# Gate rows made one by one between groups of gathered expert rows

## The chip, the core and the metric

One core of a Trainium2 chip runs one launch of the whole program. The metric is the device time of the launch in microseconds (us); a kernel is run several times and the median counts.

## The reference, cut to what matters

256 tokens of 1024 features pass a first block (a mixer and a retrieval layer) and a second block of two attention layers, with a context of 256 tokens beside them. Two pieces matter here. The retrieval layer scores 16384 experts for each token, keeps 16 for each of 8 heads, and adds up the 128 chosen rows of a table with weights:

```
idx = i1 * PEER_NKEYS + i2
act = jax.nn.gelu(jnp.einsum('tpkd,td->tpk', u_tab[idx], xb), approximate=False)
return jnp.einsum('tpk,tpkd->td', g * act, v_tab[idx])
```

And the results are added to the stream through gates, which are rows of 1024 numbers that depend on the conditioning vector alone, not on the tokens:

```
x = x + g2 * peer_ffn(h2, ...)        # first block
...
ctx = ctx + gate_c * yc               # second block, layer 0
x = x + gate[:, None] * y             # second block, layers 0 and 1
```

## The kernel before, in words

The kernel is written with a tile framework: the Python code names engines and tiles, and a scheduler sets each engine's order by its own estimate of times, except where an instruction is pinned. PE is the matmul engine, DVE, ACT and POOL the vector, scalar and general engines, SP issues the loads of weights.

The part around the change is in `peer` (L873). Its last phase works on 64 groups (`toks`, L968) of four tokens. For a group, `extract` (L984) picks each token's activations with one-hot matmuls (tile pmps) and a masked sum on DVE (tile junk, L995). `weights` (L999) makes four groups' scaled weights Z. Then POOL issues four gathers (L1035), each of 128 rows of 4 KB of the table v into a tile vrow, and PE adds them up in eight matmuls (vacc, L1041; the trace shows two passes for each, so 16), which are pinned in program order.

While the extraction runs, two groups are extracted for each group that is added up. After the extraction's last group, at group 30 of the sum (counted from 0), the activations' memory is given back, nine tiles for gathered rows are set aside (four of tag hv, five of tag gx, L1054), and the second block's own pool is opened (`open2`, L1102). From group 31 on, each group of gathers is followed by three steps of the generator `context` (L1162), which computes the second block's context side: load ctx, normalize it (squares on ACT and DVE, an inverse root on POOL named rsy_n, a scaling; L263 to L268), flip it (transposes on PE, tile nps), scale it by column into two parts (tile ch, L287 to L289, the odd pieces on POOL), and project it (L116 to L118, three passes a product, weights split into wH and wL by L78 and L79). Keys and queries then are normed (hss), placed (kk) and flipped (fps, L1321).

The eight gate rows are made by `rows2` (L1091), a generator with one row a step, each 512 wide: two for g2 of the first block and six for the second block's gates. A row needs gate values as a row across all partitions, but has them as a column for each block of 128. So `row` (L234) writes four diagonal 128 x 128 blocks on DVE (tile modR, L239, its pool has one buffer for it), sums them with a matmul against ones on PE (tile mrps, L241), and copies the sum on ACT (L243). The rows are needed late: gates at L388, where a layer's output is added, g2 at L1130, after the last group.

The second block (`block2`, L1206) runs its two layers after the last group, with the same projection code: key flips (fps<-kk) come between projection passes (acc<-xh), and for a layer's tokens POOL writes the rotated kk (L1300).

Of the kernel before, what the change touches and what calls it, by code (L numbers as in the profile page):

```python
# [44 lines left out]
class Builder:  # L45
# [827 lines left out]
    def peer(self):  # L873
        nc, tc, A = self.nc, self.tc, self.A
        R0 = 72
        with ExitStack() as es:
# [122 lines left out]
            def weights(b0, n):  # L999

                tb, q = b0 // 32, b0 % 32
                v = lambda t: t.rearrange("p (g b) -> p b g", g=4)[:, q:q + n]
                ts = slice(tb * P, (tb + 1) * P)
                w = zp.tile([P, 4, 4], F32, name="w", tag="w", bufs=2)[:, :n]
                nc.scalar.activation(w, v(act[:, ts]), AF.Gelu)
                nc.vector.tensor_tensor(w, w, v(sel[:, 1, ts]), op=ALU.mult)
                m = zp.tile([P, 4, 32], F32, name="zm", tag="zm", bufs=1)[:, :n]
                nc.vector.tensor_tensor(m, self.iota[:, None, 0:32].to_broadcast([P, n, 32]),
                                        self.iota[:, q:q + n, None].to_broadcast([P, n, 32]), op=ALU.is_equal)
                Z = zp.tile([P, 4, 4, 32], F32, name="Z", tag="Z", bufs=2)[:, :n]  # L1010
                nc.vector.tensor_tensor(Z, m[:, :, None, :].to_broadcast([P, n, 4, 32]),
                                        w[:, :, :, None].to_broadcast([P, n, 4, 32]), op=ALU.mult)
                return Z
# [11 lines left out]
            for b0, n in chunks:  # L1025
                while done < b0 + n and next(ex, True) is None:
                    done += 1
                Z = weights(b0, n)
                for b in range(b0, b0 + n):
                    tb, ts = toks[b]  # L1030
                    V = []
                    for t in ts:
                        c = tb * P + t
                        v = next(places)("vrow", F32)
                        nc.gpsimd.indirect_dma_start(  # L1035
                            v, None, rows, bass.IndirectOffsetOnAxis(ap=at[:, c:c + 1], axis=0))
                        V.append(v)

                    for dh in range(2):
                        for g in (3, 2, 1, 0):  # L1040
                            tc.keep_in_program_order(nc.tensor.matmul(  # L1041
                                out[2 * tb + dh][32 * g:32 * g + 32], Z[:, b - b0, g],
                                V[g][:, dh * 512:(dh + 1) * 512], start=b % 32 == 0, stop=b % 32 == 31,
                                tile_position=(0, 32 * g)))
                    if ctx is None:
                        for _ in range(2):
                            if next(ex, True) is None:
                                done += 1
                        if done == 64:
                            next(ex, None)  # L1050
                            eb.close()
                            ea.close()
                            gx = pool("gx", e2)
                            places = cycle([hv] * 4 + [spare(gx, "gx", 5)] * 5)  # L1054
                            self.mod_pool(gx, 1, 1)
                            rows2 = self.rows2()
                            self.open2()
                            self.run(rows2)
                            ctx = self.context()
                    else:  # L1060
                        for _ in range(3):
                            next(ctx, None)
            self.run(ctx)
# [618 lines left out]
```

## Time and profile before

| | us |
|---|---|
| runs, lowest / median / highest | 1569.92 / 1570.83 / 1579.71 |
| profiled execution, its time | 1572.23 |
| profiled execution, its span | 1570.5 |

The span is what the trace covers; the execution's own time is 1.7 us longer. PE works 1449.7 us of the span (92%), DVE 922.3, ACT 694.6, POOL 387.4. A share of the whole span says little here, since the stages have different limits: the question is what each engine does around the eight rows, and what ends each wait there. In a timeline each row is a stretch of equal instructions with its start, its length and, in brackets, the idle time ahead of it and what ended that.

### The profile page before, as it was taken

What the parts mean: (1) busy time and instruction counts of PE and PEld (TensorE: products, weight loads), DVE (VectorE), ACT (ScalarE), POOL (GpSimd) and SP (SyncE); (2) the same over time, 40 slices, a digit from 0 to 9 for tenths busy, and PEclk for the clock granted to TensorE, in tenths of its full rate; (3) what the DMA queues carried; (4) which work ended last, traced back from release to release, by engine and by line L of the source; (5) the groups of instructions that cost most, each with busy time, mean ns of one, the idle gap of its engine ahead of it and who ended that gap; (6) DMA issues with size and microseconds to landing.
All of it is one profiled execution on the core that took longest, in us unless ns stands there. A gap on an engine that the chain in (4) does not pass through costs nothing. (4 is left out here: it accounts for less than half of the span.)

```text
span 1570.5 us, 26116 instructions
## 1 busy us (share of the span) xinstructions
PE 1449.7 (92%) x10090; PEld 1126.8 (72%) x10090; DVE 922.3 (59%) x2284; ACT 694.6 (44%) x1152; POOL 387.4 (25%) x380
## 2 busy tenths in 40 slices
PE   7999987899999999999999996787969789998998
PEld 3677764799888899999877774253735458867876
DVE  4468464579998444444355554344334478866975
ACT  4354232444444455555444443222323355655563
POOL 1100101000000000000366663256576735012301
PEclk9999997899999999999899998698989899999999
DMA  9535244356877856656699998379997956414521
GB/s 352 165 133 188 83 143 134 123 167 212 309 277 262 297 180 188 188 189 189 228 346 349 350 342 309 148 269 334 365 336 276 328 187 201 155 54 149 187 75 40
DMA packets 97179, 345.80 MB, mean 220 GB/s; under 512 B 12704, under 2 KB 14240, under 8 KB 95776
## 3 DMA queue, kind: packets, MB, share of 16 engines
q1 hardware_dynamic: 54576, 198.73, 37.5%
q0 software_dynamic: 36864, 134.23, 23.3%
q10 hardware_dynamic: 5616, 11.18, 2.2%
q8 instruction: 79, 1.29, 0.3%
q14 instruction: 44, 0.36, 0.1%
HBM read 343.05 MB, written 1.05 MB: 219 GB/s over the span
## 5 line engine op out<-in xcount | busy, mean ns | idle before, releaser
L79 DVE TENSOR_TENSOR wL<-raw,wH 128x1024 fp32r<-128x1024 f32 x269 | 334.0, 1242 | 254.7 <-ACT wH L78 253.4
L78 ACT CAST wH<-raw 128x1024 fp32r<-128x1024 f32 x277 | 290.3, 1050 | 376.5 <-PE ups L117 148.5
L1035 POOL DMA_INDIRECT vrow<-in_v_dram,at x256 | 255.3, 997 | 626.4 <-DMA raw<-in_u_dram 436.7
L116 PE MATMUL ups<-h2T,wH 128*128 128x256 f32 x1024 | 287.7, 281 | 0.0
L118 PE MATMUL ups<-h2T,wL 128*128 128x256 f32 x1024 | 286.4, 281 | 0.0
L117 PE MATMUL ups<-h2T,wH 128*128 128x256 f32 x1024 | 285.6, 279 | 0.0
L116 PEld LDWEIGHTS ups<-h2T,wH 128*128 128x128 f32 x1024 | 192.5, 188 | 14.3 <-ACT ATa L921 6.7
L118 PEld LDWEIGHTS ups<-h2T,wL 128*128 128x128 f32 x1024 | 192.1, 188 | 8.4 <-DVE tkc L826 1.7
L117 PEld LDWEIGHTS ups<-h2T,wH 128*128 128x128 f32 x1024 | 192.5, 188 | 0.0
L1041 PE MATMUL vacc<-vrow,Z 128*32 128x512 f32 x1024 | 143.8, 635 | 16.6 <-DMA vrow<-in_v_dram,at 16.5
L995 DVE SCALAR_TENSOR_TENSOR junk<-iota,sel,pmps 128x128 f32<-128x128 f32 x256 | 89.0, 348 | 96.2 <-PE pmps L992 89.4
L992 PE MATMUL pmps<-ATa,oh 128*128 128x72 f32 x512 | 104.8, 287 | 1.8 <-ACT oh L981 1.8
L992 PE MATMUL pmps<-ATb,oh 128*128 128x56 f32 x512 | 98.1, 274 | 0.0
L1041 PEld LDWEIGHTS vacc<-vrow,Z 128*32 128x32 f32 x1024 | 29.2, 113 | 79.0 <-issue 50.6
L980 ACT ACTIVATE oh<-farps,place 128x512 f32<-128x512 f32 x64 | 43.9, 687 | 86.6 <-PE farps L977 84.0
L992 PEld LDWEIGHTS pmps<-ATa,oh 128*128 128x128 f32 x512 | 80.2, 198 | 2.0 <-ACT oh L981 2.0
L992 PEld LDWEIGHTS pmps<-ATb,oh 128*128 128x128 f32 x512 | 80.3, 198 | 1.7 <-issue 1.7
L211 PE MATMUL modps<-mraw,condP 128*32 128x512 f32 x192 | 44.1, 682 | 17.3 <-DMA mraw<-in_w_mod_dram 8.6
L1480 ACT ACTIVATE smp<-sps,smst 128x512 f32<-128x512 f32 (+1 forms) x72 | 44.5, 620 | 33.1 <-DVE smst L1478 27.7
L921 ACT COPY ATa<-ups 128x256 f32<-128x256 f32 x72 | 47.5, 660 | 21.6 <-PE ups L118 21.5
L1478 DVE TENSOR_REDUCE smst<-sps 128x1 f32<-128x512 f32 (+1 forms) x72 | 42.3, 596 | 14.1 <-PE sps L1474 13.7
L116 PE MATMUL acc<-wL,xh 128*128 128x512 f32 (+1 forms) x128 | 47.9, 374 | 2.8 <-ACT wH L78 2.8
(407 smaller groups left out, 2949.2 us busy)
## 6 DMA issues: line engine op xcount, KB each, us to landing
raw<-in_u_dram SPq DMA_DIRECT2D x128, 512.0 KB, 3.7
mraw<-in_w_mod_dram SPq DMA_DIRECT2D x96, 512.0 KB, 5.2
raw<-in_w_in_dram SPq DMA_DIRECT2D x40, 512.0 KB, 4.5
raw<-in_w_out_dram SPq DMA_DIRECT2D x32, 512.0 KB, 3.6
raw<-in_w_gate_dram SPq DMA_DIRECT2D x24, 512.0 KB, 4.2
raw<-in_peer_wq_dram SPq DMA_DIRECT2D x16, 512.0 KB, 3.6
vrow<-in_v_dram,at POOLq DMA_INDIRECT x256, 6.3
raw<-in_w_nv_dram SPq DMA_DIRECT2D x8, 512.0 KB, 4.6
```

The costliest lines, as they stand in the source:

```text
L78: self.pin(nc.scalar.copy(H, raw))
L79: self.pin((low or nc.vector).tensor_sub(L, raw, H.bitcast(F32)))
L116: mm(ps, a[0], b[1], start=start, stop=False)
L117: mm(ps, a[0], b[0], start=False, stop=False)
L118: mm(ps, a[1], b[0], start=False, stop=stop)
L211: nc.tensor.matmul(ps[g:g + 32], cond[:, k], raw[k // 2][:, k % 2 * 512:(k % 2 + 1) * 512], start=k < 4, stop=k >= 4, tile_position=(0, g))
L921: nc.scalar.copy(acts[0][:, :, i1] if i1 < R0 else acts[1][:, :, i1 - R0], ps)
L992: nc.tensor.matmul(pm[:, i, r0:r1], oh[:, i], a[:, tb * P + t], start=True, stop=True)
L995: nc.vector.scalar_tensor_tensor(junk, self.iota, sel[:, 0, c:c + 1], pm[:, i], op0=ALU.is_equal, op1=ALU.mult, accum_out=act[:, c:c + 1])
L1035: nc.gpsimd.indirect_dma_start(v, None, rows, bass.IndirectOffsetOnAxis(ap=at[:, c:c + 1], axis=0))
L1041: tc.keep_in_program_order(nc.tensor.matmul(out[2 * tb + dh][32 * g:32 * g + 32], Z[:, b - b0, g], V[g][:, dh * 512:(dh + 1) * 512], start ...
L1480: nc.scalar.activation(p, ps, AF.Exp, bias=st[:, 0:1], accum_out=st[:, 1:2])
```

## The change

The generator `rows2` was run to its end at group 30; now it is only made there, and takes one step after each group from 31 on, ahead of the three steps of `context`. After eight groups it is used up.

```diff
                             self.mod_pool(gx, 1, 1)
                             rows2 = self.rows2()
                             self.open2()
-                            self.run(rows2)
                             ctx = self.context()
                     else:
+                        next(rows2, None)
                         for _ in range(3):
                             next(ctx, None)
```

On PE, after the last one-hot product (pmps), stood all eight rows (mrps), then group 31 (vacc), the flips of the context (nps), group 32 and the projection (acc<-ch):

```order
L992 MATMUL pmps<-ATb,oh 128x56
L241 MATMUL mrps<-modR,one 128x512 x8
L1041 MATMUL vacc<-vrow,Z 32x512 x8
L278 MATMUL nps<-ident,ctx_9869 128x128 x8
L1041 MATMUL vacc<-vrow,Z 32x512 x8
L278 MATMUL nps<-ident,ctx_9869 128x128 x8
L116 MATMUL acc<-wL,ch_9888 128x512
```

Now at the same place of PE's order:

```order
L992 MATMUL pmps<-ATb,oh 128x56
L241 MATMUL mrps<-modR,one 128x512
L1041 MATMUL vacc<-vrow,Z 32x512 x8
L278 MATMUL nps<-ident,ctx_9813 128x128 x4
L241 MATMUL mrps<-modR,one 128x512
L278 MATMUL nps<-ident,ctx_9813 128x128 x8
L1041 MATMUL vacc<-vrow,Z 32x512 x8
L278 MATMUL nps<-ident,ctx_9813 128x128 x4
L116 MATMUL acc<-wL,ch_9832 128x512
```

One row stays ahead of group 31, the second stands among the flips. The third and fourth come within the projection's passes, the next four around groups 34 to 36 and the flips of kk, of which the eighth row stands after group 36.

On POOL, in the same stretch, the gathers (vrow) stand with the context's inverse root (rsy_n) and the odd pieces of its scaling (ch):

```order
-L1035 DMA vrow<-in_v_dram,at 128x1024 x133
+L1035 DMA vrow<-in_v_dram,at 128x1024 x137
 L68 TENSOR_TENSOR rsy_n<-rsx_n,half 128x2
-L1035 DMA vrow<-in_v_dram,at 128x1024 x8
-L289 TENSOR_TENSOR ch_9889<-nhf,ch_9888 128x256 x3
+L1035 DMA vrow<-in_v_dram,at 128x1024 x4
+L289 TENSOR_TENSOR ch_9833<-nhf,ch_9832 128x256 x4
```

Four gathers have moved from behind the inverse root to ahead of it; the pieces of ch now have four gathers between them and the root, where there were eight.

On PE, in the first layer of the second block, the first flips of the keys (fps<-kk) stood after 108 projection passes of that block (acc<-xh), two of twelve, and the other ten after 120:

```order
L118 MATMUL acc<-wH,xh_12088 128x512
L1321 MATMUL fps<-ident,kk 128x128 x2
L116 MATMUL acc<-wL,xh_12087 128x512
L117 MATMUL acc<-wH,xh_12087 128x512
L118 MATMUL acc<-wH,xh_12088 128x512
```

Now eight of them stand after 96 passes, and the last four after 120:

```order
L118 MATMUL acc<-wH,xh_12088 128x512
L1321 MATMUL fps<-ident,kk 128x128 x8
L116 MATMUL acc<-wL,xh_12087 128x512
L117 MATMUL acc<-wH,xh_12087 128x512
L118 MATMUL acc<-wH,xh_12088 128x512
```

The code there is the same as before; the scheduler has placed the flips 12 passes earlier. The second layer differs in the same way.

## Rows read from the trace of the kernel before

**Rows 1.** Busy time by stretch; start:end, length, engines, clock, DMA share, GB/s

```profile
core 0: us, PE busy (x) PEld busy (x) DVE busy (x) ACT busy (x) POOL busy (x), PEclk, DMA share, GB/s
978.00:982.00 4.00, 1.72 (x2) 0.50 (x2) 3.11 (x13) 0.00 (x0) 0.00 (x0) 0.50 1.03 425
984.60:1006.20 21.60, 15.85 (x35) 4.31 (x34) 7.32 (x26) 5.88 (x10) 1.69 (x2) 0.51 0.00 1
1006.20:1040.00 33.80, 23.79 (x128) 12.40 (x126) 15.46 (x31) 9.91 (x21) 22.75 (x23) 0.95 0.93 331
1040.00:1273.00 233.00, 196.79 (x1134) 113.12 (x1134) 100.49 (x209) 74.98 (x158) 147.76 (x133) 0.92 0.86 312
1273.00:1570.00 297.00, 274.57 (x1722) 225.49 (x1721) 227.19 (x424) 163.15 (x313) 58.17 (x52) 0.98 0.39 125
```

**Rows 2.** PE's timeline, 965 to 1008 us: start, length, instructions, idle before

```profile
965.90 0.37 PE L992 MATMUL pmps<-ATb,oh 128*128 128x56 f32 x2
971.18 2.05 PE L241 MATMUL mrps<-modR,one 128*128 128x512 f32 x2 [4.90 <-DVE modR L239]
...
996.25 2.04 PE L241 MATMUL mrps<-modR,one 128*128 128x512 f32 x2 [1.06 <-DVE modR L239]
999.35 2.04 PE L241 MATMUL mrps<-modR,one 128*128 128x512 f32 x2 [1.06 <-DVE modR L239]
1001.32 3.64 PE L1041 MATMUL vacc<-vrow,Z 128*32 128x512 f32 x16
1004.89 1.44 PE L278 MATMUL nps<-ident,ctx 128*128 128x128 f32 x8
1006.26 1.92 PE L1041 MATMUL vacc<-vrow,Z 128*32 128x512 f32 x16
```

**Rows 3.** POOL's timeline, 1005 to 1018 us

```profile
1005.24 1.45 POOL L1035 DMA_INDIRECT vrow<-in_v_dram,at  x1 [18.40 <-PE vacc L1041]
...
1008.24 0.94 POOL L1035 DMA_INDIRECT vrow<-in_v_dram,at  x1 [0.30 <-PE vacc L1041]
...
1015.42 2.35 POOL L289 TENSOR_TENSOR ch<-nhf,ch 128x256 fp32r<-128x256 f32 x3
```

**Rows 4.** ACT's timeline, the context's load and scaling

```profile
971.41 0.67 ACTq L1170 DMA_DIRECT2D ctx<-in_ctx_dram  x1
...
986.87 1.15 ACT L268 ACTIVATE ctx<-ctx,rsy_n 128x1024 f32<-128x1024 f32 x1 [0.74 <-POOL rsy_n L68]
```

**Rows 5.** The tile ctx, 960 to 1015 us, its two loads

```profile
DMA to landing us min/median/max: 8.0/10.5/13.1
```

**Rows 6.** DVE's timeline, 982 to 986 us

```profile
982.37 0.87 DVE L239 TENSOR_SCALAR modR<-ident,gc 128x128 f32<-128x128 f32 x4 [1.18 <-PE mrps L241]
984.51 1.22 DVE L264 SCALAR_TENSOR_TENSOR ch<-ctx 128x1024 fp32r<-128x1024 f32 x1 [1.27 <-DMA ctx<-in_ctx_dram]
```

**Rows 7.** PE's timeline, 1016 to 1038 us

```profile
1016.21 1.22 PE L118 MATMUL acc<-wH,ch 128*128 128x512 f32 x2 [4.24 <-POOL ch L289]
...
1033.60 1.91 PE L1041 MATMUL vacc<-vrow,Z 128*32 128x512 f32 x12 [2.09 <-DMA vrow<-in_v_dram,at]
1037.27 0.41 PE L1321 MATMUL fps<-ident,kk 128*128 128x128 f32 x2 [1.76 <-DVE kk L1305]
```

**Rows 8.** PE's waits, 1040 to 1273 us: total, times, longest

```profile
PE vacc L1041 <- DMA vrow<-in_v_dram,at: 14.4, 8, 3.7
```

**Rows 9.** PE's timeline, projection passes 97 of the second block's layers

```profile
1312.01 0.39 PE L116 MATMUL acc<-wL,xh 128*128 128x512 f32 x1
...
1453.73 0.39 PE L116 MATMUL acc<-wL,xh 128*128 128x512 f32 x1
```

**Rows 10.** POOL's timeline, the keys kk of both layers

```profile
1312.14 1.56 POOL L1300 TENSOR_TENSOR kk<-raw,rot 128x256 f32<-128x256 f32 x1 [1.16 <-DVE raw L1298]
1314.00 1.06 POOL L1300 TENSOR_TENSOR kk<-raw,rot 128x256 f32<-128x256 f32 x1 [0.29 <-DVE raw L1298]
...
1455.81 1.05 POOL L1300 TENSOR_TENSOR kk<-raw,rot 128x256 f32<-128x256 f32 x1 [0.29 <-DVE raw L1298]
```

## Prediction

> **What bounds the kernel now.** I read the busy time by stretch first, then the timelines of the five engines around the eight rows, then PE's waits to the end. [...] In the steady part a row comes every 3.10 us (996.25 to 999.35 by the start of PE's rows): DVE's four products wait for PE's matmul, as there is one buffer, and PE's matmul for them. Behind the rows stand the gathered group 31 (vacc, 1001.3) and the flips of the context (nps, 1004.9). POOL has nothing to gather meanwhile: its next gather waited 18.40 us for that vacc [rows 3].
>
> [...] The flips need the normalized context: its load was issued at 971.4, landed 13.1 us later [rows 4, 5], its squares start at 984.5, and the scaling on ACT ends at 986.87 + 1.15 = 988.0 [rows 4, 6]. So the flips could have begun at 988.0 and began at 1004.9: 16.9 us are the rows'. After 1273 PE works 274.6 of 297 us [rows 1], so that the end of the kernel is PE's.
>
> **What the change removes.** Seven of eight rows leave this place. The first stays, then comes vacc of group 31, then half the flips, the second row and the rest (the order of PE). POOL's order tells more: four gathers more, those of group 33, stand ahead of the context's power (rsy_n). They need only vacc 31, which now runs at about 973.2 to 977 (3.64 us at the lower clock, [rows 2]); four issues at 0.94 + 0.30 us [rows 3] end at about 982, before the power's input is there, so the power itself isn't late. But they put 4 x 128 rows of 4 KB = 2.1 MB into DMA engines that are full, at 425 GB/s 4.9 us of work [rows 1], while the context is loading. The load so lands between 0 and 4.9 us later. The trace has two loads of this tile, 8.0 and 13.1 us [rows 5]; I take 3.0, a little over the middle, as the queues are full at that time. The flips then start at 991.0, and 13.9 us are won here (bounds 12.0 and 16.9).
>
> [...]
>
> **What it adds behind the flips.** The second row's 2.05 us stands between the flips, and DVE writes the third row's diagonal (0.87 us, [rows 6]) before its first affine piece; against this POOL now has four gathers, not eight, between vacc 32 and the odd pieces of ch for which PE waited 4.24 us until 1016.2 [rows 3, 7]. Before, PE went on 11.3 us after the first flip. Now: twelve flips at 1.44 us for eight and the second row are 4.2 us, vacc 32 1.92 to 3.64 [rows 2], four issues 5.0, the first of POOL's three pieces 0.8 [rows 3], together 11.9 to 13.7. Loss 0.6 to 2.4; I take 1.5.
>
> **The other six rows.** [...] vacc takes 3.64 us at the lower clock and 1.92 at the higher [rows 2], so I estimate a row at 2.05 x 1.92 / 3.64 = 1.08 us. Rows five to seven stand where PE waits anyway, for vrow and for kk (2.09 + 1.76 us, [rows 7]), and I cost them at nothing; if that cover is gone they cost 3.2. Rows three, four and eight stand among projection passes on a busy PE: 3 x 1.08 = 3.2 us. From 1040 to 1273 PE has 36 us idle, 14.4 of them waits for gathers [rows 1, 8], so even these may hide.
>
> **What it moves far behind.** The scheduler orders the second block anew, in both layers in the same way. Before, the flips of kk (fps) came as 2 after 108 projection passes and 10 after 120; now 8 come after 96. There the passes run unbroken: pass 97 starts at 1312.01 [rows 9]. But POOL writes the first kk from 1312.14 to 1313.70 and the second until 1315.06 [rows 10]. So PE, which didn't wait here, now waits 1.7 us at least and 3.05 at most; 1315.06 is the nearer for eight flips, of which the first six go as soon as the first key is there, so 2.2. The second layer has the same picture (pass at 1453.73, second kk until 1456.86, [rows 9, 10]). Two layers: 4.4 us lost, bounds 0 (if DVE's order, which changed too, brings kk earlier) and 6.1.
>
> **The sum.** Against the profiled execution, 1572.23 us: -13.9 + 1.5 + 3.2 + 4.4 = -4.8, so 1567.4. The profiled execution is 1.4 us above the median of the runs shown (1570.83), so a run should give 1566.0. All bounds together: from 16.9 - 0.6 = 16.3 us faster to 12.0 - 2.4 - 12.3 - 6.1 = 8.8 us slower. About 1% of this kernel, 15.7 us, is what a measurement can tell from no change; the forecast is within it.
>
> **Rivals.** One, DMA sets the end of the gathering phase. For: share 0.93 and 0.86 after the hole [rows 1]. Then rows on PE cost nothing, and what counts is the closed hole: 4.9 us of gathers go ahead of time, and gathering resumes after vacc 32, at about 997 and not 1006.2, so 14.1 us; with an undelayed context 17.1, and if the second block loses nothing the time is 1553.7. Against: PE is busy 196.8 of 233 us in the same stretch [rows 1], and gathers wait for its vacc, so both bind in turn.
>
> Two, the alternation moves along with the rows. Each moved row still needs the one buffer, so DVE stands still until PE has done the row before, and in DVE's queue stand the affine pieces, the weight splits and kk; PE stands still for the diagonal. For: 3.10 us for a row now, and the context's squares on DVE begin behind a diagonal [rows 2, 6]. If all six cost 3.10, that is 18.6 us, and 12.4 - 18.6 - 6.1 = 12.3 slower: 1583. It decides from (12.4 - 4.4) / 6 = 1.3 us a row on. Against: projection passes or a gathered group lie between most of the rows now, so that the row before is mostly done when the next diagonal is due. [...]
>
> Three, that nothing moves, because the scheduler puts the rows together again, is out: the order has them at eight places.
>
> **How the numbers follow.** Forecast 0.62, DMA 0.24, alternation 0.14. The second reaches beyond 15.7 us only with the early context, more than half of its chance: 0.14 faster by over 1%. The third passes 15.7 us slower only with a new wait besides, or a slower clock: 0.06. The rest, 0.80, is within 1%. The range for 8 in 10 reaches from the DMA case, 1553, to near the worst of the sum, 1577.
>
> **What would show it.** The hole in DMA shrinks to some 8 us and lies before about 997. The flips start at 988 to 993 and the ch passes after the wait at about 1003. The gathered phase ends 9 us before 1273, and the second block, counted from its first projection pass, is 4 us longer, with a wait for kk at its first fps. Wrong would be a context that lands after 990, rows that each cost PE over 1.3 us, or a second block as long as before; a gain above 15.7 us would say that DMA was the bound and PE's order worth nothing.

## The result, and the profile after

The kernel before took 1572.59 us (median of 5 runs, 1569.92 to 1579.71), the changed kernel 1553.83 us (median of 5, 1545.91 to 1554.30). The ratio is 0.9871, its 95% interval 0.9841 to 0.9900: faster by 1.3%, or about 20 us. The forecast was 4.8 us, no change that can be measured; the time lies just inside its range, whose lower end (1553) was put there for rival one and not by the sum, and the largest wrong term came out with the other sign.

The profiled execution of the changed kernel is its fastest one, 1545.91 us with a span of 1544.0. 6.1 of the 26.5 us between the two spans lie ahead of the change, where the order of every engine is the same in both traces (the last one-hot product ends at 960.2, before at 966.3). So all that follows is counted from the end of that product: 604.2 us to the end before, 583.8 after, 20.4 less, near what the ratio says.

First the busy time by stretch of the changed kernel, columns as in [rows 1]:

```profile
978.00:982.00 4.00, 2.32 (x6) 1.48 (x7) 0.75 (x1) 1.15 (x1) 0.73 (x1) 0.50 1.02 415
982.00:986.00 4.00, 4.00 (x21) 2.03 (x23) 2.51 (x8) 2.52 (x5) 0.00 (x0) 0.56 0.16 64
986.00:990.00 4.00, 3.38 (x21) 2.09 (x14) 2.17 (x5) 1.58 (x3) 2.42 (x3) 1.00 0.39 113
990.00:994.00 4.00, 2.86 (x10) 1.40 (x10) 1.84 (x4) 0.75 (x2) 3.68 (x5) 1.00 0.99 410
960.20:1265.00 304.80, 243.93 (x1373) 137.34 (x1373) 143.62 (x313) 105.86 (x211) 177.82 (x163) 0.91 0.83 302
1265.00:1544.00 279.00, 263.53 (x1648) 217.68 (x1648) 217.02 (x405) 151.88 (x296) 53.40 (x50) 0.98 0.40 127
```

And the last two of these stretches in the kernel before:

```profile
966.30:1287.40 321.10, 250.77 (x1372) 139.76 (x1372) 140.24 (x311) 104.78 (x207) 178.93 (x163) 0.88 0.79 287
1287.40:1570.50 283.10, 265.53 (x1648) 217.07 (x1648) 218.47 (x407) 153.49 (x300) 56.77 (x50) 0.97 0.39 125
```

The hole of 21.6 us in the DMA share, 0.00 from 984.6 to 1006.2 us [rows 1], has shrunk to the 8 us from 982 to 990, with shares of 0.16 and 0.39. The phase, from the last one-hot product to the second block's first projection pass, is 16.3 us shorter: PE works 6.9 us less in it (the same instructions, at granted clock 0.91 and not 0.88) and is idle 9.5 us less. The second block is 4.1 us shorter.

PE's timeline of the changed kernel answers to [rows 2, 7]:

```profile
964.11 2.05 PE L241 MATMUL mrps<-modR,one 128*128 128x512 f32 x2 [3.95 <-DVE modR L239]
966.09 3.06 PE L1041 MATMUL vacc<-vrow,Z 128*32 128x512 f32 x16
979.68 1.09 PE L278 MATMUL nps<-ident,ctx 128*128 128x128 f32 x4 [10.54 <-DVE ctx L267]
980.56 1.92 PE L241 MATMUL mrps<-modR,one 128*128 128x512 f32 x2
...
990.69 1.10 PE L241 MATMUL mrps<-modR,one 128*128 128x512 f32 x2 [0.24 <-DVE nhf L288]
992.69 0.74 PE L118 MATMUL acc<-wH,ch 128*128 128x512 f32 x2 [0.90 <-POOL ch L289]
...
1003.71 1.02 PE L241 MATMUL mrps<-modR,one 128*128 128x512 f32 x2
```

The flips start 19.5 us after the last one-hot product; before it was 38.6. In their place PE now waits 10.54 us for the context. The first row takes 2.05 us at a granted clock of 0.50. From the third row on, a row takes 1.02 to 1.13 us at a clock of 1.00, but for one of 1.31 us, around which the clock was 0.70 (1015 to 1017 us).

POOL's timeline answers to [rows 3], ACT's and the tile ctx to [rows 4, 5]:

```profile
978.06 0.73 POOL L68 TENSOR_TENSOR rsy_n<-rsx_n,half 128x2 f32<-128x2 f32 x1 [2.83 <-DVE rsx_n L67]
986.97 1.01 POOL L1035 DMA_INDIRECT vrow<-in_v_dram,at  x1 [8.18 <-PE vacc L1041]
...
991.89 2.37 POOL L289 TENSOR_TENSOR ch<-nhf,ch 128x256 fp32r<-128x256 f32 x3
```

```profile
964.29 0.45 ACTq L1170 DMA_DIRECT2D ctx<-in_ctx_dram  x1
...
978.82 1.15 ACT L268 ACTIVATE ctx<-ctx,rsy_n 128x1024 f32<-128x1024 f32 x1 [1.21 <-POOL rsy_n L68]
```

```profile
DMA to landing us min/median/max: 12.1/12.1/12.1
```

POOL's wait for vacc fell from 18.40 to 8.18 us, and the context landed 12.1 us after its issue, before 13.1. Last, the waits of PE from the last one-hot product to the second block (total, times, longest), first of the kernel before, then of the changed one:

```profile
PE mrps L241 <- DVE modR L239: 18.8, 8, 7.1
PE vacc L1041 <- DMA vrow<-in_v_dram,at: 16.5, 9, 3.7
PE nps L278 <- DVE ctx L256: 7.7, 1, 7.7
PE fps L1321 <- DVE kk L1305: 5.5, 6, 1.8
PE poolps L1429 <- DMA band<-in_band_dram: 4.6, 1, 4.6
PE acc L118 <- POOL ch L289: 4.2, 1, 4.2
PE fps L1321 <- DVE raw L1305: 2.7, 1, 2.7
```

```profile
PE vacc L1041 <- DMA vrow<-in_v_dram,at: 26.8, 9, 5.7
PE nps L278 <- DVE ctx L267: 10.5, 1, 10.5
PE fps L1321 <- DVE kk L1305: 4.7, 4, 1.8
PE mrps L241 <- DVE modR L239: 4.0, 1, 4.0
...
PE poolps L1429 <- DMA band<-in_band_dram: 1.5, 1, 1.5
...
PE fps L1321 <- DVE raw L1305: 1.0, 1, 1.0
PE acc L118 <- POOL ch L289: 0.9, 1, 0.9
```

The reader should add these by place. In front (rows, first context, ch): 18.8 + 4.2 = 23.0 before, 4.0 + 10.5 + 0.9 = 15.4 after: only 7.6 us less, since the exposed context took most of what the rows gave up. Behind (the context's later chain: fps for kk and raw, the load band, the second norm ctx L256; and the gathers): 20.5 + 16.5 = 37.0 before, 7.2 + 26.8 = 34.0 after. The chain's waits fell by 13.3 us and the gathers' rose by 10.3; I read this as PE waiting for the one or the other around the same groups, so that only the sum counts. With the 6.9 us of PE's work these make 17.5 us less, and waits elsewhere are 1.1 us longer, which leaves the 16.3 within rounding.

### The profile page after: what moved, and what is told of

It is laid out like the page before. It is cut to its first block, busy times and chain, and to the rows that moved or that the text cites. A ratio compares the mean times of both kernels' runs of the same rounds, so it can differ in the third digit from the quotient of the medians.

```text
span 1544.0 us, 26118 instructions
## 1 busy us (share of the span) xinstructions
PE 1436.1 (93%) x10090; PEld 1122.3 (73%) x10090; DVE 924.0 (60%) x2284; ACT 693.7 (45%) x1152; POOL 383.1 (25%) x380
## 4 chain that ended last, share of the span: by engine, by line
PE 86%; DMA 4%; DVE 4%; POOL 2%; issue 2%; ACT 2%; ACTq 0%; POOLq 0%; DVEq 0%
PE acc L116 10%; PE acc L118 10%; PE acc L117 9%; PE ups L116 8%; PE ups L118 8%; PE ups L117 8%; PE pmps L992 7%; PE vacc L1041 7%; PE modps L211 4%; DMA vrow<-in_v_dram,at 2%; PE tps L1491 2%; PE pvo L1497 2%; POOL vrow L1035 1%; PE mcps L231 1%; PE farps L977 1%
## 5 line engine op out<-in xcount | busy, mean ns | idle before, releaser
L116 PEld LDWEIGHTS ups<-h2T,wH 128*128 128x128 f32 x1024 | 192.5, 188 | 14.3 <-issue 5.0
L1041 PE MATMUL vacc<-vrow,Z 128*32 128x512 f32 x1024 | 147.4, 647 | 26.8 <-DMA vrow<-in_v_dram,at 26.8
L980 ACT ACTIVATE oh<-farps,place 128x512 f32<-128x512 f32 x64 | 43.9, 687 | 87.0 <-PE farps L977 87.0
L211 PE MATMUL modps<-mraw,condP 128*32 128x512 f32 x192 | 43.5, 677 | 16.5 <-DVE condP L186 8.3
L1478 DVE TENSOR_REDUCE smst<-sps 128x1 f32<-128x512 f32 (+1 forms) x72 | 42.5, 597 | 18.8 <-PE sps L1474 18.2
```

Source lines behind the costliest of these rows:

```text
L116: mm(ps, a[0], b[1], start=start, stop=False)
L211: nc.tensor.matmul(ps[g:g + 32], cond[:, k], raw[k // 2][:, k % 2 * 512:(k % 2 + 1) * 512], start=k < 4, stop=k >= 4, tile_position=(0, g))
L1041: tc.keep_in_program_order(nc.tensor.matmul(out[2 * tb + dh][32 * g:32 * g + 32], Z[:, b - b0, g], V[g][:, dh * 512:(dh + 1) * 512], start ...
```

## The experiments

Sixteen runs on other chips, four at a time. There the kernel before takes 1608.01 us (first four), 1608.12 and 1608.61 (second and third four, on one chip) and 1575.92 (last four), so ratios to before on the same chip are compared. In the table, "flip" is the time from the last one-hot product to the first flip of the context and "phase" that to the second block's first pass; "work" is PE's busy time in the phase, "front" and "behind" are its waits there by the two sums above, with all their small rows; "block" is from that pass to the end. These are of one profiled execution each. What work, front and behind leave of the phase, 9.3 to 17.8 us, are waits outside the two sums. The largest single one, where it shows, is at the phase's end, for the flips of the normalized stream that the second block starts from (nps<-fxn): 1.5 us in the kernel before, none in the changed kernel, 7.5 in e1, e2, e3, e6 and e7, 9.9, 9.2 and 9.6 in e12, e11 and e14.

| run | ratio, 95% | flip | phase | work | front | behind | block |
|---|---|---|---|---|---|---|---|
| before (first chip) | 1 | 38.6 | 321.2 | 250.8 | 23.2 | 37.0 | 283.1 |
| changed (first chip) | 0.9871, 0.9841 to 0.9900 | 19.5 | 304.8 | 243.9 | 16.2 | 34.0 | 279.0 |
| a2_again | 0.9838, 0.9790 to 0.9886 | 21.6 | 307.7 | 245.6 | 18.9 | 31.5 | 279.6 |
| e1_lean_after | 0.9861, 0.9818 to 0.9903 | 19.4 | 311.4 | 244.6 | 16.6 | 33.8 | 277.9 |
| e2_lean_before | 0.9879, 0.9839 to 0.9918 | 19.2 | 306.1 | 240.8 | 15.6 | 33.4 | 281.3 |
| e3_before_2buf | 0.9897, 0.9855 to 0.9940 | 27.3 | 314.6 | 249.0 | 15.9 | 32.0 | 278.6 |
| e5_bunch | 0.9966, 0.9945 to 0.9986 | 18.6 | 321.3 | 247.3 | 17.4 | 45.3 | 280.1 |
| e6_two | 0.9900, 0.9874 to 0.9925 | 21.5 | 315.2 | 245.8 | 16.9 | 35.6 | 278.1 |
| e4_ctx_pool | 0.9875, 0.9841 to 0.9910 | 16.5 | 307.2 | 246.6 | 13.7 | 33.2 | 278.4 |
| e7_after_2buf | 0.9880, 0.9842 to 0.9918 | 16.6 | 302.9 | 244.0 | 10.0 | 31.1 | 277.8 |
| b2_before | 0.9994, 0.9962 to 1.0027 | 36.1 | 329.9 | 254.4 | 21.5 | 40.0 | 282.4 |
| e8_bunch_2buf | 0.9885, 0.9823 to 0.9946 | 18.7 | 311.5 | 245.8 | 11.3 | 43.3 | 282.7 |
| e10_late_spread | 0.9932, 0.9906 to 0.9958 | 20.2 | 322.9 | 248.6 | 14.3 | 43.9 | 279.8 |
| e9_pool_2buf | 0.9841, 0.9791 to 0.9891 | 16.8 | 305.2 | 244.3 | 9.8 | 41.5 | 278.5 |
| e12_after_noroot | 0.9876, 0.9835 to 0.9918 | 21.3 | 300.6 | 235.7 | 19.9 | 28.6 | 283.5 |
| e11_late_noroot | 0.9823, 0.9769 to 0.9877 | 21.4 | 307.3 | 245.6 | 17.0 | 30.3 | 279.3 |
| e13_bunch_noroot | 0.9884, 0.9813 to 0.9955 | 20.4 | 308.1 | 245.1 | 19.3 | 34.4 | 281.2 |
| e14_before_noroot | 0.9889, 0.9848 to 0.9930 | 38.5 | 312.0 | 246.4 | 23.1 | 27.2 | 281.0 |

**What the rows cost.** The changed kernel again, both kernels without rows two to eight, and the kernel before with two buffers for the diagonals. The edit of e1 and e2 (the same for the second half of g2) and that of e3:

```diff
-                self.row(g[:, d], cols)
+                self.nc.scalar.copy(g[:, d], self.one.to_broadcast([P, 512]))
```

```diff
...
-        d = self.mp.tile([P, 4, P], F32, name="modR", tag="mraw", bufs=self.nmraw)
+        pool, tag, n = self.rowbuf or (self.mp, "mraw", self.nmraw)
+        d = pool.tile([P, 4, P], F32, name="modR", tag=tag, bufs=n)
...
-                            rows2 = self.rows2()
+                            rows2, self.rowbuf = self.rows2(), (zp, "oh", 2)
```

> The changed kernel once more, for its profile and its time. If the gain is the closed hole and the shorter second block, both come again: the context's flips start 19 us after the last one-hot product (38.6 in the kernel before), the second block's first projection pass 305 us after it (321 before), and the second block, from that pass to the end, takes 279 us (283 before); ratio to the kernel before 0.987. If part of it is the chance of one profiled execution, the first two come again and the second block takes 283.

> The changed kernel with rows two to eight made without DVE's diagonals and PE's matmuls: ACT alone writes ones in place of the gate values (a part of the computation left out). Theory one, moved rows cost PE nothing since gathers set the pace: time within 2 us of the changed kernel, ratio 0.986 to 0.988. Theory two, as in the prediction, moved rows cost PE about 1.1 us each where it is busy: 3 to 8 us faster than the changed kernel, ratio 0.982 to 0.985. Its scheduler order has the key flips after 96 passes in the second block's first layer and after 108 and 120 in its second layer: if the place of the flips makes a layer shorter, the first takes 138.7 us and the second 142.4.

> The kernel before, all rows in one place, with rows two to eight made without DVE's diagonals and PE's matmuls (ACT writes ones in place of the gate values; this part is left out). It is what is to be had from this place at most. Theory one: as fast as the changed kernel within 2 us, ratio 0.986 to 0.988, with the context's flips at 18 to 20 us after the last one-hot product. Theory two: 3 to 8 us faster than the changed kernel.

> The kernel before, all eight rows in one place, but the diagonals go to two buffers (the one-hot tiles' memory, free by then) and not one, so that DVE writes the next while PE multiplies. If the alternation of DVE and PE makes the hole, a row comes every 2.05 us and not 3.10: the flips start 7 us earlier, 31 us after the last one-hot product, ratio 0.995. If the alternation isn't what counts (PE waits for something else at the first rows), less than 3 us are won, ratio above 0.998.

The gain repeats (0.9838). Taking seven rows out of the changed kernel brings nothing that can be measured (0.9861), so there they cost nothing that shows. Out of the kernel before it brings about what the change brings (0.9879): in one go at that place they cost some 1.2%. With two buffers a good part of that is gone though the rows stay in one place (0.9897, interval 0.9855 to 0.9940). That is more than either expectation had (0.995, or above 0.998): the flips came 11.3 us earlier than in the kernel before, not 7. So much of the rows' price there goes with the alternation of DVE and PE over one buffer, 3.10 us a row [rows 2]. How much is not shown, since the order moved elsewhere too: the second block of e2 and of e3 has its first key flips after 96 passes in its first layer, as in the changed kernel, and e3's block is 278.6 us long.

**Are early flips the gain?** In all of these the flips come earlier too. Four variants of the changed kernel part the two: all rows in one go behind group 40, two rows a step, the context's load from POOL's queue, and two buffers (the edit of e3).

```diff
-                        next(rows2, None)
+                        if b == 40:
+                            self.run(rows2)
```

```diff
                         next(rows2, None)
+                        next(rows2, None)
```

```diff
-        load = lambda: self.nc.scalar.dma_start(ctx, A["ctx_2"])
+        load = lambda: self.nc.gpsimd.dma_start(ctx, A["ctx_2"])
```

> The changed kernel, but all eight rows are made in one go behind group 40 of the sum, so that they stand on PE in a bunch around groups 39 to 41 and not one by one. Theory one (what the change gains is that the flips of the context come earlier; where the rows are made later is free, as the gathers set the pace there): the flips start some 17 to 19 us after the last one-hot product, as in the changed kernel, and the time is 0.983 to 0.989 of before. Theory two (the rows gain because they are spread, so that their diagonals hide behind other PE work): the bunch costs PE up to 8 x 1.6 = 12 us in its new place, and the time is 0.991 to 0.996 of before.

> The changed kernel with two rows a step, so that the rows are used up after four groups. Theory one (free places): 0.983 to 0.989 of before, the flips at most 2 us later than in the changed kernel. Theory two (each row near the flips delays them, since it stands ahead of the context's work on DVE and PE): the flips and the first passes over ch come 4 to 7 us later and the time is 0.987 to 0.992.

> The changed kernel, but the load of the context is issued from POOL's queue, between the gathers, and not from ACT's. Theory one (the flips wait for this load, and the gathering phase ends as much earlier as they start): if it is issued some 8 us earlier, the flips start 8 to 10 us after the last one-hot product and the time is 0.979 to 0.983 of before. Rival (the flips no longer set the end of the phase; the gathers do): the flips start earlier and the time stays at 0.985 to 0.988. Third, the load stands behind four gathers on POOL and lands no earlier: flips and time as in the changed kernel.

> The changed kernel with two buffers for the diagonals of the rows in place of one. Theory one (moved rows are free): no change against the changed kernel, 0.983 to 0.989 of before. Theory two (in the new places a diagonal still waits for the matmul of the row before, and DVE's queue with it): 2 to 5 us faster than the changed kernel, 0.981 to 0.984 of before.

The bunch refuted theory one: flips at 18.6 us, and yet 0.9966, just beyond the far end of theory two. There is no hole in its DMA share either: it is 0.83 to 0.97 from 1084 to 1100 us, where six of the rows stand. Two stretches of these:

```profile
1088.00:1092.00 4.00, 2.94 (x16) 0.66 (x12) 1.88 (x7) 0.81 (x2) 2.34 (x3) 1.00 0.83 274
1092.00:1096.00 4.00, 2.91 (x18) 0.64 (x18) 1.89 (x8) 1.17 (x2) 3.08 (x4) 1.00 0.92 334
```

Its waits in front are as short as in the changed kernel, and those behind 45.3 us, more than in any other run. The waits at the rows themselves (mrps) are 5.9 us in all; the longest waits are:

```profile
PE vacc L1041 <- DMA vrow<-in_v_dram,at: 20.2, 6, 6.3
PE fps L1322 <- DVE kk L1306: 11.6, 5, 5.2
PE nps L278 <- DVE ctx L267: 9.6, 1, 9.6
PE fps L1322 <- DVE raw L1306: 7.3, 1, 7.3
PE poolps L1430 <- DMA band<-in_band_dram: 6.2, 1, 6.2
```

Nor did flips 5.1 us earlier than in the repeat, with the load from POOL's queue, shorten the phase (307.2 against 307.7), and two buffers bring nothing more (0.9880). Two rows a step are at 0.9900, between the two: the flips and the first pass that waits for ch (33.3 us after the product, 34.0 in the repeat) come no later, so theory two's reason does not hold, though its range does.

**Bunch, place, or buffer?** The kernel before again, the bunch with two buffers, the rows one by one from group 40 on, and two buffers with the load from POOL's queue as an attempt at a faster kernel.

```diff
-                        next(rows2, None)
+                        if b >= 40:
+                            next(rows2, None)
```

> The kernel before, unchanged, so that its profile stands on the same chip as the others. Its second block (first projection pass to the end) took 283.1 us in the first profile, 279.0 and 279.6 in the two profiles of the changed kernel. Theory one (the order of the flips of kk sets that): 282 to 284 again. Rival (it is a dip of the granted clock that comes and goes): 278 to 281. The rest: last one-hot product to the first flip some 38 us, to the second block some 321 to 326.

> All eight rows in one bunch behind group 40, as in the run of that kind before (0.9966), but with two buffers for their diagonals. If the bunch's price is that PE and DVE wait for each other over the one buffer: most of it goes, 0.986 to 0.991 of before. If its price is its place (what stands behind it in DVE's and PE's queues comes later, whatever the buffer): 0.994 to 0.998.

> The changed kernel, its rows one by one as there, but from group 40 on and not from group 31 on. Flips as early as with the bunch behind group 40. If what counts is that rows stand one by one, each beside a gathered group: 0.984 to 0.989 of before, as the changed kernel. If it is the place behind group 40 that costs: 0.994 to 0.998, as the bunch there.

> The changed kernel with two buffers for the diagonals and the load of the context issued from POOL's queue, an attempt at a faster one. If PE's work is the bound of the phase and earlier flips bring nothing more: 0.984 to 0.989 of before, as the changed kernel. If the two edits add up: 0.978 to 0.983.

Two buffers mend a good part of the bunch (0.9885, as the first answer had it). How much is not settled: the interval is wide, 0.9823 to 0.9946, and three of its four runs, 1594.7 to 1597.2 us, are 0.991 to 0.993 of the median before. The waits behind stayed at 43.3 us there, and e9 has 41.5 in a phase of 305.2 us, so that column alone does not say which kernel is slow. Late rows one by one lie between the two answers at 0.9932. The attempt at a faster kernel is not faster than the changed one. One place where the late rows lose shows in three timelines of e10, POOL's, DVE's and PE's:

```profile
1106.91 0.94 POOL L1035 DMA_INDIRECT vrow<-in_v_dram,at  x1 [3.15 <-PE vacc L1041]
...
1109.39 0.94 POOL L1035 DMA_INDIRECT vrow<-in_v_dram,at  x1 [0.31 <-issue]
1110.35 1.67 POOL L68 TENSOR_TENSOR hss<-hss,half 128x8 f32<-128x8 f32 x1
```

```profile
1101.65 0.16 DVE L67 TENSOR_SCALAR hss<-hss 128x8 f32<-128x8 f32 x1
1101.73 1.22 DVE L79 TENSOR_TENSOR wL<-raw,wH 128x1024 fp32r<-128x1024 f32 x1
1112.06 0.76 DVE L1276 TENSOR_TENSOR raw<-acc,hss 128x256 f32<-128x256 f32 x2 [9.12 <-POOL hss L68]
```

```profile
1113.29 0.66 PE L1322 MATMUL fps<-ident,raw 128*128 128x128 f32 x2 [6.65 <-DVE raw L1306]
```

The inverse root of the norms (hss, on POOL) has its input at 1101.81 and starts at 1110.35: in POOL's queue stand gathers ahead of it, and one of these waits 3.15 us for PE's vacc. DVE waits 9.12 us for it and PE 6.65. In the changed kernel this root stands behind gathers too, and DVE waits 6.26 us for it; but PE meanwhile stands at a gathered group, 5.68 us, and then finds raw ready:

```profile
1070.36 0.75 DVE L1275 TENSOR_TENSOR raw<-acc,hss 128x256 f32<-128x256 f32 x2 [6.26 <-POOL hss L68]
```

```profile
1070.64 3.64 PE L1041 MATMUL vacc<-vrow,Z 128*32 128x512 f32 x16 [5.68 <-DMA vrow<-in_v_dram,at]
1074.21 0.66 PE L1321 MATMUL fps<-ident,raw 128*128 128x128 f32 x4
```

So the root's delay and the gather's fall together there, and e10 meets them one after the other. With the group ahead of these (a wait of 1.82 us in the changed kernel, 2.76 in e10) PE waits 7.5 us at this place in the changed kernel and 9.4 in e10. This makes 1.9 of the 15.2 us between the phases of e10 and the repeat (322.9 and 307.7); what the other places add is not shown.

**Without the root in POOL's queue.** Four kernels, with one edit more:

```diff
-        nc.gpsimd.tensor_tensor(y, x, self.half[:, :n], op=ALU.pow)
+        if pool:
+            nc.gpsimd.tensor_tensor(y, x, self.half[:, :n], op=ALU.pow)
+        else:
+            nc.vector.tensor_tensor(y, x, self.half[:, :n], op=ALU.mult)
```

> The changed kernel without the inverse root of the keys' and queries' norms on POOL: a multiplication of the same shape on DVE stands in its place, so that nothing of the second block's norms stands among the gathers in POOL's queue. It is the base for the three others. Both theories: faster than the changed kernel by up to the root's own wait, 0.972 to 0.986 of before.

> Rows one by one from group 40 on, without that root on POOL. Theory one (rows made one by one are free anywhere, and the late ones lost their gain to the root behind the gathers): within 0.003 of the changed kernel without the root. Theory two (the late place itself costs): 0.006 to 0.010 above it, as with the root.

> All eight rows in a bunch behind group 40, without that root on POOL. Theory one (the bunch costs what PE works and waits in it, some 15 us, of which a part hides as PE would have waited for gathers): 0.003 to 0.007 above the changed kernel without the root. Theory two (the bunch stays as dear as it was, 0.011 above): 0.009 to 0.013.

> The kernel before without that root on POOL. If the change's gain comes from the rows' place and from nothing that the root does in POOL's queue, the distance to the changed kernel without the root is again 0.012 to 0.016. If part of the gain was an earlier root, it is 0.004 to 0.010.

The four are alike within their intervals: 0.9876, 0.9823, 0.9884, 0.9889. The changed kernel gains nothing from it, where both theories had 0.972 to 0.986; the late rows gain 0.011 (0.9932 to 0.9823), the bunch 0.008, the kernel before 0.011. These gains compare ratios from two chips, and the changed kernel with the root did not run on the chip of these four; on the two chips where it ran its ratios are 0.003 apart. So with the root out of the way late rows cost nothing that shows, and of the bunch's price at most a part is left (the difference is 0.0008 ± 0.008, below theory one's 0.003 to 0.007, and theory two's 0.009 is at its edge). Above all, the kernel before now has the changed kernel's time, though its rows wait as ever (in front 23.1 us) and its flips start 38.5 us after the product. What it lost are waits behind, 27.2 us where they were 37.0 and 40.0, and some of PE's work, 246.4 us where it was 250.8 and 254.4; 8.1 us came back as the wait at the phase's end (fxn, 9.6 for 1.5). PE's longest wait in the phase is still the rows':

```profile
PE mrps L244 <- DVE modR L242: 18.6, 8, 6.2
```

The distance between before and changed kernel is 0.0013 ± 0.006 here, below the 0.004 to 0.010 of an earlier root as part of the gain, with an interval that reaches 0.007; one profile of each has 592.9 and 584.1 us behind the one-hot product, 8.8 apart. So by this interval the rows' place by itself is worth at most some 11 of the 20 us; the rest showed only together with the root in POOL's queue. The order of PE and DVE changes with this edit too, so that it is not the root's wait alone that was taken away.

## Why the prediction was wrong, step by step

**Right.** A row at the higher clock was put at 1.08 us and took 1.02 to 1.13 at a granted clock of 1.00, and 1.31 where that was 0.70. The hole was to shrink to some 8 us and did. The loss behind the flips, 1.5 us: from the first flip to the pass that waited for POOL's ch it was 11.3 us, and is 992.69 - 979.68 = 13.0, so 1.7. That the second row stands between the flips and POOL has four gathers there was read from the order, and held.

**Wrong by 8.5 us: the second block, +4.4.** This is the step that failed most. It said that PE waits for kk, since POOL writes the keys from 1312.14 on [rows 10] and the flips move to pass 97 [rows 9]. But that time belongs to DVE's and POOL's order of before. In the changed kernel DVE's sums and POOL's keys moved as well; counted from the block's first pass (1287.4 and 1265.0), the sums come at 13.1 us where they came at 18.5, and the first key at 18.6 where it came at 24.7. The sums before:

```profile
1305.94 1.12 DVE L1268 TENSOR_REDUCE hss<-raw 128x2 f32<-128x128 f32 x4
```

And after, with the keys and their flips:

```profile
1278.07 1.31 DVE L1268 TENSOR_REDUCE hss<-raw 128x2 f32<-128x128 f32 x4 [0.62 <-ACT raw L1267]
...
1283.56 0.74 POOL L1300 TENSOR_TENSOR kk<-raw,rot 128x256 f32<-128x256 f32 x1 [0.94 <-DVE raw L1298]
...
1288.51 1.04 PE L1321 MATMUL fps<-ident,kk 128*128 128x128 f32 x8
```

The flips wait for nothing, in the second layer either. The bound "0, if DVE's order brings kk earlier" was named and not looked into, though the order was there to read, and it even was too high. The block is 4.1 us shorter. Half of that is the first layer, counted up to the flips of the second layer's input (nps<-nxn): 140.7 and 141.4 us with the order of before (two profiles), 138.7 and 139.0 with that of the changed kernel. The second layer took 142.4 and 141.0 us before, 140.3 and 140.7 after, and there the granted clock differed in one stretch, from 236 to 240 us of the block: 0.63 in the first profile of before (1523.4 to 1527.4 us), 1.00 in that of the changed kernel (1501 to 1505 us). The kernels e1 and e2 have the first layer's key flips as in the changed kernel and the second's as in the kernel before: their first layers took 137.3 and 139.0 us, and their second 140.6 and 142.3, where 142.4 was expected of e1. So the rest of the 4.1 us is not settled, and theory one's 282 to 284 for b2 (282.4) is the order's only in part.

**Wrong by 5.0 us: the context's load, "3.0 later".** It landed 12.1 us after its issue, not 13.1 + 3.0 = 16.1, and was issued 4.1 us after the one-hot product where it was 5.1. (In the repeat a2 it was issued 5.3 us after the product, and its squares start 13.1 us after the issue, as in the kernel before: no delay there either, but about 2 of the 5.0 us belong to the one profile.) So at the pass that waits for ch the gain was 17.4 us, where 13.9 - 1.5 = 12.4 stood. Four gathers were issued from 969.41 to 975.2, while it was under way and the DMA share was 1.01. They did not come on top of what the load met before. The gathers' queue (packets, MB, share of the 16 engines) from the load's issue to its landing, in the kernel before and in the changed one, and in the changed one from then to 986 us:

```profile
q0 software_dynamic: 578, 2.08, 39.3%
```

```profile
q0 software_dynamic: 570, 2.06, 45.5%
```

```profile
q0 software_dynamic: 638, 2.29, 58.5%
```

In both kernels the load shared the engines with as many bytes of gathers, 2.08 and 2.06 MB, and after it had landed the queue of the changed kernel still moved 2.29 MB, where the four gathers are 2.1; whether these are the four's bytes is not shown. So the 13.1 us of before, to which the term added 3.0, were measured beside gathers already, and that four more of them delay the load by 3.0 us was an estimate of mine that no run bears out. The trace of the changed kernel has the queues on the engines side by side: from 969.4 to 972 us the queue of the load had a share of 51.0%, the gathers' 28.6% and the weights' 22.2%. In which order single packets went is not shown here.

**Wrong by 2.1 us: three rows at 1.08, 3.2.** From that pass to the second block it was 271.2 us before and is 272.3 after, so all rows and all else there cost 1.1, and the run without rows (e1) says that rows cost nothing that shows. That six rows cost at most 2.05 us each, the 12.3 us in the sum's worst case, no run shows as a bound; in the changed kernel the third to the eighth took 6.8 us. The sum of the three errors is 15.6, from -4.8 to -20.4.

**The rivals.** Rival one has the right time (1553.7; 14 to 17 us in the phase, rows free), but its reason does not stand alone, and that the time agrees is in part luck, since it put the second block at nothing, which gave 4.1 us. It let the closed hole in DMA decide, and the sign that I named for it, a gain above 15.7 us, came without DMA being the bound. The bunch behind group 40 has early flips (18.6 us after the product), a DMA share of 0.83 to 0.97 around its rows, and hardly a gain; the kernel before without the root has late flips (38.5 us), group 31 (vacc) 34.9 us after the product, where the kernel before has it after 35.0 with the hole ahead of it, and nearly the whole gain. What the runs show instead: PE stands at waits that its fixed order sets, in front (rows, first context) and behind, where POOL's roots stand among gathers, and the phase is PE's work, the sum of both and 9 to 18 us of other waits. The change takes from the first three; an earlier start in front is lost again where the order behind makes PE meet the root's delay and the gathers' one after the other, as one place of e10 shows. That the scheduler's new order far from the edit would take part in the gain, in the phase and in the second block, the prediction did not weigh in this direction. Rival two, the alternation that moves along, is out for the changed kernel (mrps waits 4.0 us in all, at the first row), but right in part for the bunch: there PE waited 5.9 us at the rows, at a granted clock of 1.00 (1084 to 1100 us), with two buffers 0.2 (e8). That is less than the bunch loses against the changed kernel, so its waits behind count too.

What stays open: how much of the gain in the kernel as it is comes from the rows and how much from the root's place, since with the root the two cannot be parted by an edit that leaves the scheduler's order alone; no run fixed that order by hand.

## What to carry to other kernels

Where a scheduler or a pool sets the order, an edit moves more than its own lines: read the order of all engines that feed a wait, not of the waiting one alone, and don't take a producer's time from the old trace when its queue was reordered too. A small operation that stands in its engine's order among transfers that wait for another engine can cost several times its length (here a root of 1.7 us, which started 6.1 and 8.5 us after its input); its distance from its input's end is the number to look up. And before a closed gap is called the gain, make one kernel with the gap closed and no gain, or with the gain and the gap open.

## What the runs showed of the hardware

A load of 1 MB on ACT's queue shared the DMA engines with gathers and weights and took about as long in both kernels: 13.1 us beside 2.08 MB of gathers in the kernel before, 12.1 us beside 2.06 MB in the changed one, where four gathers more were issued 5 to 10 us behind it. An inverse root of 1.7 us on POOL started 6.1 and 8.5 us after its input (changed kernel, e10): three or four gathers were issued ahead of it, and one of these had waited 1.92 and 3.15 us for PE's vacc. And a row took PE 2.05 us in the kernel before, at a granted clock of 0.50 (971.2 to 1001.4 us), and 1.02 to 1.13 us in the changed kernel where the clock was 1.00: the third to the eighth row, one of them at 0.70, took 6.8 us where six took 12.3, which is most of the 6.9 us that PE works less.
